# Seven block products for eight in both FFN projections of a two-layer encoder, token-major, with weight sums built by adding DMAs

## The chip, the cores and the metric

One Trainium2 chip, one core of it. The metric is device time in microseconds (us) of one execution; a kernel's time is the median of its runs. The engines named below are TensorE (PE in the profile; its weight loads are PEld), VectorE (DVE), ScalarE (ACT), GpSimd (POOL) and SyncE (SP, which issues the plain DMAs).

## The reference

A trunk of two layers on x of 512 tokens by 1024 channels, in float32. Each layer is a half-step SwiGLU FFN, a token mixer, and a second half-step FFN; a final RMSNorm ends it.

```python
def swiglu(h, w_in, w_out):                       # w_in 1024 x 5632, w_out 2816 x 1024
    gate, up = jnp.split(h @ w_in, 2, axis=-1)
    return (jax.nn.silu(gate) * up) @ w_out

for l in range(DEPTH):                            # DEPTH = 2
    x = x + 0.5 * swiglu(rms_norm(x, ffn1_norm[l]), ffn1_w_in[l], ffn1_w_out[l])
    x = x + token_mixer(rms_norm(x, mix_norm[l]), w_in[l], ...)
    x = x + 0.5 * swiglu(rms_norm(x, ffn2_norm[l]), ffn2_w_in[l], ffn2_w_out[l])
return rms_norm(x, final_norm)
```

The mixer projects x by a 1024 x 5376 matrix to three branches (pooling, differential attention, a gated linear recurrence) and their gates, merges the branches, and projects by a 1024 x 1024 matrix.

## The kernel before

Activations are channel-major: `x[m]` is 128 channels by 512 tokens. A float32 product is made of three TensorE matmuls in the 32-bit rounded type (fp32r): every operand is split into a high part (a rounding copy on ACT, `zh`, `wh`, `hh`) and a low part (source minus high part on DVE, `zl`, `wl`, `hl`), and `mm3` adds high x high, high x low and low x high into one PSUM bank.

The program is a list of **units**. A unit is 128 x 1024 weights (`raw`, loaded by SP in blocks of 128 x 2048), split into `wh` and `wl`, and the matmuls that use them: the weights are the stationary operand, 128 x 128 at a time, and the 512 tokens stream past, so a full unit has 8 x 3 = 24 matmuls of 512 columns. An FFN has 44 units for the input projection (a gate and an up tile of 128 columns in turn) and 24, some of them with 7 for 8 tiles, for the output projection. The last FFN's output projection (`final_proj`) is token-major, so that the result needs no transposing.

The order on each engine is the order in which the code emits it. After the matmuls of unit i, `gap` emits the delayed DVE work (`flush`), then the unit's own work on its result (`after`), then the ACT half of the split of unit i+3 (`splits_to`), side work of the mixer, and last the DVE half of that split, behind which the next block's DMA is issued (`loads`). So a unit's weights are split while the three units ahead of it run.

The norm factor `R` (one per token) is not applied to z but to the results; it is made from squares added up over the channel tiles and one matmul with a matrix of ones (`norm_R`, tile `nrm`).

Of the kernel before, what the change touches and what calls it, by code (L numbers as in the profile page):

```python
# [44 lines left out]
SLOTS = 72  # L45
# [3 lines left out]
SCQ = 2  # L49


class Block:
    def __init__(self, load):
        self.load = load
        self.raw = None
# [27 lines left out]
class Unit:  # L83
    def __init__(self, block, view, mm, after, nk=8, cost=5.2, shape=None):
        self.block = block
        self.view = view
        self.mm = mm
        self.after = after
        self.nk = nk
        self.cost = cost  # L90
        self.shape = shape or [8, 128]
        self.hi = self.lo = None
        self.late = 0
        self.group = 2
        self.ahead = False
# [3 lines left out]
def trunk_kernel(ctx, tc, xT, pm, fin, cst, bd, f1i, f1o, win, wbp, wba, wbl, wout, f2i, f2o, out):  # L99
    nc = tc.nc  # L100
    V, A, PE, SP = Counted(nc.vector, 0.075, 0.00104), Counted(nc.scalar, 0.14, 0.00083), Counted(nc.tensor, 0.0, 0.00042), nc.sync

    cp_ = ctx.enter_context(tc.tile_pool(name="const", bufs=1))
    sp = ctx.enter_context(tc.tile_pool(name="slots", bufs=SLOTS))
    rp = ctx.enter_context(tc.tile_pool(name="raw", bufs=3))
    wp = ctx.enter_context(tc.tile_pool(name="whl", bufs=3))
    dp = ctx.enter_context(tc.tile_pool(name="pad", bufs=2))
# [3 lines left out]
    def slot(dt=F32, name="s"):  # L111
        return sp.tile([128, S], dt, tag="s", name=name)

# [16 lines left out]
    def hilo(src, name):  # L130

        hi, lo = slot(F32R, name + "h"), slot(F32R, name + "l")
# [28 lines left out]
    x = [None] * KD  # L161
    st = {}

    def z_chunk(m, gain):

        z_split(m, gain)
        sq_chunk(m)

    def z_split(m, gain):
        zh, zl = slot(F32R, "zh"), slot(F32R, "zl")  # L170
        A.activation(out=zh, in_=x[m], func=AF.Copy, scale=gain(m))
        V.scalar_tensor_tensor(out=zl, in0=x[m], scalar=gain(m), in1=f(zh), op0=MUL, op1=SUB)
        st["z"][m] = (zh, zl)

    def sq_chunk(m):
        if m == 0:
            st["acc"] = slot(name="acc")
            A.activation(out=st["acc"], in_=x[m], func=AF.Square)
        else:
            q = slot(name="sq")  # L180
            A.activation(out=q, in_=x[m], func=AF.Square)
            V.tensor_tensor(out=st["acc"], in0=st["acc"], in1=q, op=ADD)
# [7 lines left out]

    def inv_rms(acc, n, eps, col):
        return rsqrt_newton(*inv_rms_start(acc, n, eps, col))
# [11 lines left out]
    def norm_R():  # L204
        st["R"] = inv_rms(st.pop("acc"), D, EPS, 0)

    units = []
    hooks = {}

    def add_hook(i, fn):  # L210
        hooks.setdefault(i, []).append(fn)


    def blk(pieces):
        def load(raw):
            for dst, src in pieces:
                SP.dma_start(out=dst(raw), in_=src)
        return Block(load)

    def cols_block(w, c0, n=256):  # L220
        return blk([(
            lambda raw: raw[:, 0:8 * n].rearrange("p (k f) -> p k f", f=n),
            w[:, c0:c0 + n].rearrange("(k p) f -> p k f", p=128),
        )])

    def col_view(s, n=256, k=8, c=128):
        return lambda raw: raw[:, 0:k * n].rearrange("p (k f) -> p k f", f=n)[:, :, s * c:(s + 1) * c]

    def zmm(get_bank, nk=KD, src="z"):

        def mm(u, k0, k1):
            if k0 == 0:
                get_bank(True)
            acc = get_bank(False)
            for k in range(k0, k1):
                zh, zl = st[src][k]
                mm3(acc, u.hi[:, k * 128:(k + 1) * 128], u.lo[:, k * 128:(k + 1) * 128], zh, zl, k == 0, k == nk - 1)
        return mm
# [9 lines left out]
    def ffn(l, wi, wo, next_gain, last, first=None):  # L248
        h = [None] * KF

        def pair(j, bg, bu, s):
            box, bx2 = {}, {}

            def after_gate():
                g, th = slot(name="g"), slot(name="th")
                V.tensor_tensor(out=g, in0=box["ps"], in1=st["R"], op=MUL)
                A.activation(out=th, in_=g, func=AF.Tanh, scale=0.5)
                r = st["R"]

                def rest():  # L260
                    V.scalar_tensor_tensor(out=g, in0=th, scalar=1.0, in1=g, op0=ADD, op1=MUL)
                    V.tensor_tensor(out=g, in0=g, in1=r, op=MUL)

                later.append(rest)
                box["g"] = g

            def after_up():
                g = box["g"]
                V.tensor_tensor(out=g, in0=bx2["ps"], in1=g, op=MUL)
                h[j] = hilo(g, "h")  # L270

            if bg is None:
                return (box, after_gate), (bx2, after_up)
            units.append(Unit(bg, col_view(s), zmm(new_bank_fn(box)), after_gate))
            units.append(Unit(bu, col_view(s), zmm(new_bank_fn(bx2)), after_up))

        if first is not None:
            for s in range(2):
                first.extend(pair(s, None, None, s))
        for jj in range(0 if first is None else 1, KF // 2):  # L280
            bg, bu = cols_block(wi, jj * 256), cols_block(wi, DFF + jj * 256)
            pair(2 * jj, bg, bu, 0)
            pair(2 * jj + 1, bg, bu, 1)

        if last:
            final_proj(wo, h)
            return
        kbs = [(0, 8), (8, 15), (15, KF)]
        for cg in range(4):
            blocks = []  # L290
            for k0, k1 in kbs:
                blocks.append(blk([(
                    lambda raw, n=k1 - k0: raw[:, 0:n * 256].rearrange("p (k f) -> p k f", f=256),
                    wo[k0 * 128:k1 * 128, cg * 256:(cg + 1) * 256].rearrange("(k p) f -> p k f", p=128),
                )]))
            boxes = [{}, {}]
            order = [(b, s) for b in range(3) for s in range(2)] if cg < 3 else [(b, s) for s in range(2) for b in range(3)]
            for b, s in order:
                k0, k1 = kbs[b]

                def mm(u, a0, a1, k0=k0, k1=k1, box=boxes[s]):
                    if k0 == 0:
                        box["ps"] = bank()
                    for k in range(k0, k1):
                        o = (k - k0) * 128
                        mm3(box["ps"], u.hi[:, o:o + 128], u.lo[:, o:o + 128], h[k][0], h[k][1], k == 0, k == KF - 1)

                def after(m=2 * cg + s, box=boxes[s], fin=b == 2):
                    if not fin:
                        return  # L310
                    if m == 0:
                        st["z"] = [None] * KD
                    V.scalar_tensor_tensor(out=x[m], in0=box["ps"], scalar=0.25, in1=x[m], op0=MUL, op1=ADD)
                    z_chunk(m, next_gain)

                n = k1 - k0
                units.append(Unit(blocks[b], col_view(s, 256, n), mm, after, nk=n, cost=0.65 * n, shape=[n, 128]))


    def final_proj(wo, h):  # L320
        xt, gain, xg = {}, {}, {}
        ss = {t: small(2) for t in range(4)}

        def prepare():
            for ch in range(2):
                gain[ch] = slot(name="fg")
                SP.dma_start(out=gain[ch], in_=fin[ch * S:(ch + 1) * S].partition_broadcast(128))
            yield 0.1, lambda: None, True
            for ch in range(2):
                for t in range(4):  # L330
                    def step(ch=ch, t=t):
                        ps = bank("xt")
                        for k in range(4):
                            PE.transpose(ps[:, k * 128:(k + 1) * 128], x[ch * 4 + k][:, t * 128:(t + 1) * 128], ident)
                        xt[t, ch] = slot(name="xt")
                        A.activation(out=xt[t, ch], in_=ps, func=AF.Copy)
                    yield 0.7, step, True

        add_hook(len(units) - 4 * (KF // 2) + 4, lambda: side.add("xt", prepare()))

        def close(t, ch, ps):
# [20 lines left out]
        for ch in range(2):  # L362
# [3 lines left out]
            for j in range(nu):  # L366
# [7 lines left out]
                def mm(u, a0, a1, j=j, ch=ch, box=box, nu=nu):  # L374
# [3 lines left out]
                    if ch == 1 and nu - tail <= j < nu - 1:  # L378
                        return
# [851 lines left out]
```

## Time and profile before

| | |
|---|---|
| median of 3 runs | 2199.44 us (2199.42 to 2199.46) |
| profiled execution, its own time | 2199.48 us |
| its span in the trace | 2197.5 us |
| TensorE busy | 2181.1 us, 99% of the span |
| VectorE busy | 1243.3 us, 57% |
| ScalarE busy | 819.6 us, 37% |
| DMA | 207 MB, 28.7% of the 16 engines' time |
| granted TensorE clock, mean | 0.999 (2.4 GHz) |

The span is what the engines' rows cover; about 2 us of the execution lie around it. Matmuls are pipelined: a row of 0.39 us follows the one ahead of it by less than that, so the cost of a matmul is read from the distance of starts, not from a row's length. Idle time of an engine that others don't wait for costs nothing.

### The profile page before, as it was taken

To read this page: it belongs to the slowest core of one execution; us is meant where nothing else is said; L and a number is where in the kernel's file an instruction comes from. 1 tells how busy PE (TensorE), PEld (TensorE's weight loads), DVE (VectorE), ACT (ScalarE), POOL (GpSimd) and SP (SyncE) were. 2 spreads that over 40 slices of the span, in tenths; PEclk is the share of its full clock that TensorE was granted. 3 is DMA by queue.
4 is the path that set the end of the run, shared out by engine and by line. 5 is a ranking of instruction groups with operands and counts; after the bars stand their busy time and mean duration, and the time that the engine had idled before them with its cause. 6 is when DMAs were issued, how large, how long until landed. Compare 5 with 4: busy or idle time off the path is not lost.

```text
span 2197.5 us, 23345 instructions
## 1 busy us (share of the span) xinstructions
PE 2181.1 (99%) x9596; PEld 1786.2 (81%) x9596; DVE 1243.3 (57%) x1743; ACT 819.6 (37%) x1137; POOL 0.2 (0%) x4
## 2 busy tenths in 40 slices
PE   9999999999999999999999999999999999999998
PEld 7888888778887888888888888877788878888887
DVE  6655434697866655543355554346977675555433
ACT  5322223645654322222232222246456443322222
POOL 0000000000000000000000000000000000000000
PEclk9999999999999999999999999999999999999999
DMA  5323232222223222232232323232222233232331
GB/s 185 113 79 115 86 103 92 96 67 87 77 68 106 96 96 96 96 106 91 91 99 93 108 84 106 87 120 73 70 87 68 89 103 106 77 115 79 113 104 50
DMA packets 193610, 207.44 MB, mean 94 GB/s; under 512 B 3808, under 2 KB 183136, under 8 KB 193504
## 3 DMA queue, kind: packets, MB, share of 16 engines
q1 hardware_dynamic: 193504, 205.96, 28.7%
q8 instruction: 75, 1.23, 0.2%
q14 instruction: 31, 0.25, 0.0%
HBM read 203.85 MB, written 2.10 MB: 94 GB/s over the span
## 4 chain that ended last, share of the span: by engine, by line
PE 87%; DVE 9%; ACT 3%; issue 1%; DMA 0%; SPq 0%; ACTq 0%; DVEq 0%
PE ps L78 74%; PE f L78 5%; PE y L78 2%; PE v L78 2%; DVE wl L78 2%; PE av L78 1%; DVE gt L78 1%; ACT wh L78 1%; PE sc L78 1%; DVE hs L78 1%; DVE tl L78 1%; DVE kl L78 1%; PE wT L78 0%; PE nrm L78 0%; DVE pw L78 0%
## 5 line engine op out<-in xcount | busy, mean ns | idle before, releaser
L78 PE MATMUL ps<-zh,wh 128*128 128x512 f32 x2016 | 793.5, 394 | 0.4 <-DVE m L78 0.2
L78 PE MATMUL ps<-zh,wl 128*128 128x512 f32 x2016 | 786.0, 390 | 2.3 <-DVE wl L78 2.0
L78 PE MATMUL ps<-zl,wh 128*128 128x512 f32 x2016 | 784.7, 389 | 0.0
L78 DVE TENSOR_TENSOR wl<-raw,wh 128x1024 fp32r<-128x1024 f32 (+1 forms) x382 | 459.8, 1206 | 289.7 <-ACT wh L78 286.3
L78 ACT ACTIVATE wh<-raw 128x1024 fp32r<-128x1024 f32 (+1 forms) x382 | 394.8, 1036 | 291.2 <-PE ps L78 171.2
L78 PEld LDWEIGHTS ps<-zh,wl 128*128 128x128 f32 x2016 | 378.4, 188 | 85.1 <-DVE wl L78 6.0
L78 PEld LDWEIGHTS ps<-zh,wh 128*128 128x128 f32 x2016 | 378.5, 188 | 82.2 <-issue 3.4
L78 PEld LDWEIGHTS ps<-zl,wh 128*128 128x128 f32 x2016 | 378.6, 188 | 81.2 <-issue 3.8
L78 PE MATMUL ps<-hh,wh 128*128 128x512 f32 x528 | 205.4, 389 | 0.0
L78 PE MATMUL ps<-hl,wh 128*128 128x512 f32 x528 | 205.4, 389 | 0.0
L78 PE MATMUL ps<-hh,wl 128*128 128x512 f32 x528 | 205.4, 389 | 0.0
L78 ACT ACTIVATE hh<-g 128x512 fp32r<-128x512 f32 x88 | 55.6, 632 | 325.0 <-DVE g L78 325.0
L78 ACT ACTIVATE th<-g 128x512 f32<-128x512 f32 x88 | 55.6, 632 | 324.7 <-DVE g L78 324.7
L78 DVE TENSOR_TENSOR g<-ps,r 128x512 f32<-128x512 f32 x88 | 60.8, 691 | 151.1 <-PE ps L78 151.0
L78 DVE TENSOR_TENSOR g<-ps,g 128x512 f32<-128x512 f32 x88 | 60.9, 691 | 118.6 <-PE ps L78 118.1
L78 PEld LDWEIGHTS ps<-hh,wl 128*128 128x128 f32 x528 | 99.1, 188 | 20.7
L78 PEld LDWEIGHTS ps<-hl,wh 128*128 128x128 f32 x528 | 99.1, 188 | 20.6
L78 PEld LDWEIGHTS ps<-hh,wh 128*128 128x128 f32 x528 | 99.1, 188 | 20.4
L78 DVE SCALAR_TENSOR_TENSOR g<-th,g 128x512 f32<-128x512 f32 x88 | 61.0, 693 | 59.9 <-ACT th L78 59.8
L78 DVE TENSOR_TENSOR hl<-g,hh 128x512 fp32r<-128x512 f32 x88 | 61.0, 693 | 59.1 <-ACT hh L78 59.0
L78 ACT ACTIVATE gt<-gt,hmb 128x512 f32<-128x512 f32 x48 | 34.8, 724 | 135.3 <-DVE gt L78 131.4
L78 ACT ACTIVATE zh<-x,par 128x512 fp32r<-128x512 f32 x48 | 34.6, 721 | 134.2 <-DVE x L78 134.2
(172 smaller groups left out, 1972.6 us busy)
## 6 DMA issues: line engine op xcount, KB each, us to landing
raw<-in_f2i_dram SPq DMA_DIRECT2D x44, 1024.0 KB, 4.9
raw<-in_f1i_dram SPq DMA_DIRECT2D x42, 1024.0 KB, 4.9
raw<-in_win_dram SPq DMA_DIRECT2D x42, 1024.0 KB, 5.1
raw<-in_f1o_dram SPq DMA_DIRECT2D x16, 896.0 KB, 4.8
raw<-in_f2o_dram SPq DMA_DIRECT2D x14, 1024.0 KB, 5.0
raw<-in_f1o_dram SPq DMA_DIRECT2D x8, 1024.0 KB, 5.1
raw<-in_wout_dram SPq DMA_DIRECT2D x8, 1024.0 KB, 5.0
raw<-in_f2o_dram SPq DMA_DIRECT2D x8, 896.0 KB, 4.8
```

The costliest lines, as they stand in the source:

```text
L78: return fn(*args, **kw)
```

## The change

**Block products.** Each FFN projection is cut into 2 x 2 blocks (the tokens in halves, the summed dimension in halves, and the output columns in halves: gate and up in the input projection, channels 0 to 511 and 512 to 1023 in the output projection), and the eight block products are replaced by seven (Winograd's form of Strassen's scheme): `P1 = A11 B11`, `P2 = A12 B21`, `Q5 = S1 (B11+B12)`, `Q3 = S4 B22`, `P6 = S2 (B11+B12+B22)`, `P7 = S3 (B12+B22)`, `Q4 = A22 (B11+B12+B22+B21)`, with signs as the code has them. S1 to S4 are sums and differences of activation blocks, made on DVE. The sums of weight blocks are built in SBUF by DMAs that add to what lies there (`add_fn`, issued by GpSimd): one tile holds B11, then B11+B12, then B11+B12+B22, and then all four.

**Token-major.** The activations are now the stationary operand (128 channels by 128 tokens of a half) and 512 columns of weights stream past. A unit is still 128 x 1024 weights, but feeds 2 token tiles x 2 weight tiles x 3 = 12 matmuls, half as many as before. The input projection goes through 2816 columns in six steps (`quad`): five of 512 columns, with 7 products of 2 units each, and one of 256 columns, with 7 products of one unit each, of 24 matmuls of 256 columns. The output projection has 7 products of 6 units (the sixth half as long).

**Combining.** The products are added up on DVE and ACT as they end (`p1` to `q4` in `quad`, `o_p1` to `o_q4` behind it), tanh is taken token-major with the norm factor as a scalar per partition, and h is transposed on TensorE (`transposes`, tile `ht`) to be stationary in the output projection. x stays token-major; z is transposed from it on TensorE (`z_block`, `z_chunk`, tile `zt`). The norm factor comes from ACT squares with a running sum, without a matmul. `final_proj` and its transposes are gone, since every output projection is now token-major.

The core of the diff, in the new kernel's form:

```diff
-SLOTS = 72
+SLOTS = 20
+BIGS = 40
...
+    def add_fn(src, n, w):
+        return lambda raw: GP.dma_start(out=raw[:, 0:n * w].rearrange("p (k f) -> p k f", f=w), in_=src, accum_op=ADD)
...
+    def seven(order, nk, width, left, wap, after, chain2, held, prep=None):
...
+                if p == "P1":
+                    block = b1[n] = Block([ld(0, 0)])
+                    acc = ap(0, 1)
+                elif p == "Q5":
+                    block, acc = b1[n], ap(1, 1)
+                elif p == "P6":
+                    block, acc = b1[n], ap(1, 0)
+                elif p == "Q4":
+                    block = b1[n]
+                elif p == "P2":
+                    block = Block([ld(1, 0)])
+                elif p == "Q3":
+                    block = b2[n] = Block([ld(1, 1)])
+                    acc = ap(0, 1) if chain2 else None
+                else:
+                    block = b2[n] if chain2 else Block([ld(0, 1)], ap(1, 1))
...
+                    for tt in range(2):
+                        acc_ = box[p][tt][:, 0:width]
+                        for k in range(k0, k1):
...
+                            PE.matmul(acc_, lhsT=ah, rhs=wh, start=k == 0, stop=False)
+                            PE.matmul(acc_, lhsT=ah, rhs=wl, start=False, stop=False)
+                            PE.matmul(acc_, lhsT=al, rhs=wh, start=False, stop=k == nk - 1)
...
+            def p6(ps):
+                def rest():
+                    for tt in range(2):
+                        add(u[tt], ps[tt], u[tt])
+                        add(v[tt], v[tt], u[tt], SUB)
+                        mul(v[tt], v[tt], st["r"][tt][2], th0[tt])
...
+                later.append(rest)
+                defer(2, transposes(0, v))
...
         def low():
-            V.tensor_tensor(out=lo, in0=src, in1=f(hi), op=SUB)
-            if last_use[id(u.block)] == i:
+            for lo, src, hi in todo:
+                V.tensor_tensor(out=lo, in0=src, in1=hi, op=SUB)
...
+            if u.acc:
+                u.acc(u.block.raw[0])
+            elif last_use[id(u.block)] == i:
...
+            loads()
```

`chain2` is true in the input projection and false in the output projection. `u.acc` is called behind the DVE half of a unit's split: the add may only start when both halves of the split have read the tile, and the unit four places on in a 512-column step (two places on in the 256-column step, twelve in the output projection) reads the sum.

DVE in an FFN's input projection. Before, this is the row for one pair of units (gate, then up), from one eviction of a gate tile to the next:

```order
L78 TENSOR_TENSOR g<-ps,r 128x512 [waits PE_49]
L78 SCALAR_TENSOR_TENSOR g<-th,g 128x512 [waits Activation_49]
L78 TENSOR_TENSOR g<-g,r 128x512 [waits DVE_49]
L78 TENSOR_TENSOR wl<-raw,wh 128x1024 [waits Activation_49]
L78 TENSOR_TENSOR g<-ps,g 128x512 [waits DVE_49,PE_49]
L78 TENSOR_TENSOR hl<-g,hh 128x512 [waits Activation_49]
L78 TENSOR_TENSOR wl<-raw,wh 128x1024 [waits DMAHW0_49,Activation_49]
```

Two splits (`wl`) come with five other operations, for 48 matmuls. Now, in a 512-column step, the stretch behind product P6 (`u<-P_826`) and then P7 (`u<-P_870`):

```order
L83 TENSOR_TENSOR u<-P_826,u 128x512 [waits PE_49]
L83 TENSOR_TENSOR v<-v,u 128x512 [waits DVE_49]
L83 SCALAR_TENSOR_TENSOR v<-v,m,th 128x512 [waits DVE_49]
L83 TENSOR_TENSOR u<-P_827,u 128x512 [waits PE_49]
L83 TENSOR_TENSOR v<-v,u 128x512 [waits DVE_49]
L83 SCALAR_TENSOR_TENSOR v<-v,m,th 128x512 [waits DVE_49]
L83 TENSOR_TENSOR wl<-raw,wh 128x1024 [waits DMASW6_49,Activation_49]
L83 TENSOR_TENSOR wl<-raw,wh 128x1024 [waits DMASW7_49,Activation_49]
L83 TENSOR_TENSOR u<-P_870,u 128x512 [waits PE_49]
L83 TENSOR_TENSOR u<-u 128x512 [waits DVE_49]
```

Six dependent operations now stand between the end of a product and the split of a unit three places on, and that split waits for an adding DMA (`DMASW`). In the output projection DVE has, behind product P2 (`x<-P_2370`), the sums `c` of h blocks, their low parts `al`, and the splits of the weights in one row:

```order
L83 TENSOR_TENSOR c_2424<-h 128x1024 [waits PE_49]
L83 TENSOR_TENSOR c_2425<-c_2424,h 128x1024 [waits DVE_49]
L83 TENSOR_TENSOR wl<-raw,wh 128x512 [waits DMAHW7_49,PE_49,Activation_49]
L83 TENSOR_TENSOR al<-c_2424,ah 128x1024 [waits Activation_49]
L83 TENSOR_TENSOR wl<-raw,wh 128x1024 [waits DMASW4_49,PE_49,Activation_49]
L83 TENSOR_TENSOR c_2467<-h 128x1024 [waits PE_49]
L83 TENSOR_TENSOR c_2468<-c_2467,h 128x1024 [waits DVE_49]
L83 TENSOR_TENSOR wl<-raw,wh 128x1024 [waits DMASW5_49,Activation_49]
L83 SCALAR_TENSOR_TENSOR x<-P_2370,x 128x512 [waits PE_49]
```

Before, DVE had only the splits and the additions to x there; the five rows with `c` and `al` are new, and the splits wait for loads and adds. The third place is GpSimd's queue, which issues the adding DMAs. Before, it held no DMA; now, at the 256-column step of the first FFN, it has one chain of three adds to the tile `raw_1520` and one add to `raw_1612`, one unit per product:

```order
L366 DMA raw_1520<-in_f1i_dram 128x4x256 [waits DMAHW1_49,DVE_49]
L366 DMA raw_1520<-in_f1i_dram 128x4x256 [waits DMASW0_49,DVE_49]
L366 DMA raw_1612<-in_f1i_dram 128x4x256 [waits DMAHW3_49,DVE_49,PE_49]
L366 DMA raw_1520<-in_f1i_dram 128x4x256 [waits DMASW1_49,DVE_49]
L366 DMA raw_1640<-in_f1o_dram 128x2x512 [waits DMASW4_49,DMAHW4_49,DVE_49,PE_49]
```

Each add waits for the one ahead of it in its tile and for DVE, which has read the tile for the split. In all there are 272 such adds, 68 to an FFN, four of them in its narrow step.

## Rows read from the trace of the kernel before

**Rows 1.** The page: engines' busy time and the chain that ended last.

```profile
PE 2181.1 (99%) x9596; PEld 1786.2 (81%) x9596; DVE 1243.3 (57%) x1743; ACT 819.6 (37%) x1137; POOL 0.2 (0%) x4
PEclk9999999999999999999999999999999999999999
...
PE 87%; DVE 9%; ACT 3%; issue 1%; DMA 0%; SPq 0%; ACTq 0%; DVEq 0%
```

**Rows 2.** Waits of PE, the largest: total us, times, longest.

```profile
PE ps L78 <- DVE wl L78: 2.5, 5, 0.7
```

**Rows 3.** Windows: FFN 2 of layer 0 (input, output projection), then a mixer.

```profile
738.00:976.00 238.00, 238.00 (x1049) 196.37 (x1048) 130.44 (x158) 72.15 (x91) 0.00 (x0) 1.00 0.30 97
976.00:1096.00 120.00, 120.00 (x531) 99.38 (x530) 42.61 (x47) 32.20 (x39) 0.00 (x0) 1.00 0.30 99
...
1460.00:1824.00 364.00, 360.43 (x1583) 290.38 (x1582) 266.04 (x428) 189.84 (x286) 0.00 (x0) 1.00 0.26 83
```

**Rows 4.** Timeline of PE: start us, length; 21 matmuls, then the norm's.

```profile
368.23 0.39 PE L78 MATMUL ps<-zh,wh 128*128 128x512 f32 x1
...
372.76 0.39 PE L78 MATMUL ps<-zh,wl 128*128 128x512 f32 x1
372.99 1.02 PE L78 MATMUL nrm<-acc,cst 128*128 128x512 f32 x2
...
374.09 0.40 PE L78 MATMUL ps<-zl,wh 128*128 128x512 f32 x1
```

**Rows 5.** Timeline of PE around eight transposes, then around four.

```profile
506.72 1.03 PE L78 MATMUL wT<-cst,e 128*128 128x128 f32 x8
...
507.82 0.40 PE L78 MATMUL ps<-zl,wh 128*128 128x512 f32 x1
...
1865.44 0.60 PE L78 MATMUL xt<-cst,x 128*128 128x128 f32 x4
...
1866.11 0.39 PE L78 MATMUL ps<-zl,wh 128*128 128x512 f32 x1
```

**Rows 6.** Lines by shape, weight loads and transposes: busy us, mean ns.

```profile
L78 PEld LDWEIGHTS ps<-zh,wl 128*128 128x128 f32 x2016 | 378.4, 188 | 85.1 <-DVE wl L78 6.0
L78 PE MATMUL wT<-cst,e 128*128 128x128 f32 x128 | 16.6, 272 | 0.0
L78 PEld LDWEIGHTS wT<-cst,e 128*128 128x128 f32 x128 | 14.9, 140 | 2.1
```

**Rows 7.** Lines by shape: DVE and ACT.

```profile
L78 DVE TENSOR_TENSOR wl<-raw,wh 128x1024 fp32r<-128x1024 f32 x334 | 407.3, 1222 | 184.5 <-ACT wh L78 181.5
L78 ACT ACTIVATE wh<-raw 128x1024 fp32r<-128x1024 f32 x334 | 349.3, 1049 | 182.1 <-PE f L78 73.1 <-PE ps L78 62.0 <-issue 15.4
L78 DVE TENSOR_TENSOR g<-ps,g 128x512 f32<-128x512 f32 x88 | 60.9, 691 | 118.6 <-PE ps L78 118.1
L78 DVE SCALAR_TENSOR_TENSOR zl<-x,par,zh 128x512 fp32r<-128x512 f32 x48 | 36.0, 750 | 36.6 <-ACT zh L78 36.6
L78 ACT ACTIVATE th<-g 128x512 f32<-128x512 f32 x88 | 55.6, 632 | 324.7 <-DVE g L78 324.7
```

**Rows 8.** The page: DMA; queue's MB and share of engines; us to landing.

```profile
DMA packets 193610, 207.44 MB, mean 94 GB/s; under 512 B 3808, under 2 KB 183136, under 8 KB 193504
q1 hardware_dynamic: 193504, 205.96, 28.7%
...
raw<-in_f2i_dram SPq DMA_DIRECT2D x44, 1024.0 KB, 4.9
raw<-in_wba_dram SPq DMA_DIRECT2D x8, 512.0 KB, 3.4
```

**Rows 9.** Timeline: PE's first product, and its last.

```profile
6.67 0.42 PE L78 MATMUL ps<-zh,wh 128*128 128x512 f32 x1
...
2190.04 0.39 PE L78 MATMUL f<-wh,hl 128*128 128x512 f32 x1
```

More of the change, by code (lines that the diff above doesn't have):

```diff
@@ L158, in pcs, with add_hook, defer @@
         return par[:, o:o + PCOLS[name][1]]
[L161 to L182, printed above, removed]
+    x = {}
+    st = {"r": {}}
+    units = []
+    hooks = {}
+    tasks = {}
+    clock = {"gap": 0}
+    def add_hook(i, fn):
+        hooks.setdefault(i, []).append(fn)
+    def defer(n, fn):
+        tasks.setdefault(clock["gap"] + n, []).append(fn)
     def rsqrt_newton(y0, m):
@@ new lines, in to_ffn, with done, to_mixer @@
+    def to_ffn(gain):
+        def done(hh, kk):
+            squares(hh, kk)
+            defer(1, z_block(hh, kk, gain))
+            z_ready(hh, kk, 2)
+        return done
+    def to_mixer(gain):
+        got = set()
+        def done(hh, kk):
+            squares(hh, kk)
+            got.add((hh, kk))
+            if kk == 1 and (1 - hh, 1) in got:
+                st["z"] = [None] * KD
+                for c2 in range(2):
+                    defer(1 + c2, lambda c2=c2: [z_chunk(4 + 2 * c2 + c, gain) for c in range(2)])
+        return done
@@ new lines, in to_out, with close @@
+    def to_out(hh, kk):
+        both = squares(hh, kk)
+        if not both:
+            for tt in range(2):
+                xv = x[2 * hh + tt, kk]
+                V.tensor_tensor(out=xv, in0=xv, in1=st["fg"][kk], op=MUL)
+            return
+        def close():
+            for tt in range(2):
+                t = 2 * hh + tt
+                r = st["r"][t][0]
+                A.activation(out=x[t, 1 - kk], in_=x[t, 1 - kk], func=AF.Copy, scale=r)
+                V.scalar_tensor_tensor(out=x[t, kk], in0=x[t, kk], scalar=r, in1=st["fg"][kk], op0=MUL, op1=MUL)
+                for c in (1 - kk, kk):
+                    SP.dma_start(out=out[t * 128:(t + 1) * 128, c * S:(c + 1) * S], in_=x[t, c])
+        later.append(close)
@@ L401, in mixer @@
+    def mixer(l, side, done, between):
         g = {}
@@ L887, in mixer @@
         units[-4].ahead = True
[L890 to L901 removed]
+        units[n0].late = units[n0 + 1].late = 4
@@ L938, in trunk_kernel, with prologue @@
     side = Side()
-    def prologue(first, w):
+    def prologue(gain):
         SP.dma_start(out=par, in_=pm)
+        SP.dma_start(out=cs[:, 0:256], in_=cst[:, 0:256])
         warm = slot(F32R, "warm")
@@ L1064, in trunk_kernel, with between @@
-    blocks = []
-    for u in units:
-        if not blocks or all(b is not u.block for b in blocks[-4:]):
+    for l in range(DEPTH):
+        g1, gm, g2 = (lambda m, n=n, l=l: pc(l, n, m) for n in ("g1", "gm", "g2"))
+        order0 = ["P1" if l == 0 else "P2", "P2" if l == 0 else "P1", "Q5", "Q3", "P6", "P7", "Q4"]
+        ffn(f1i[l], f1o[l], to_mixer(gm), order0)
+        def between(gm=gm):
+            for m in range(4):
+                z_chunk(m, gm)
+            flush()
+        mixer(l, side, to_ffn(g2), between)
+        last = l == DEPTH - 1
+        n = len(units)
+        ffn(f2i[l], f2o[l], to_out if last else to_ffn(lambda m, l=l: pc(l + 1, "g1", m)), ["P2", "P1", "Q5", "Q3", "P6", "P7", "Q4"])
+        if last:
+            add_hook(len(units) - 44, load_gains)
@@ L1067, in trunk_kernel, with loads @@
+    blocks, last_use = [], {}
+    for i, u in enumerate(units):
+        if u.block and id(u.block) not in last_use:
             blocks.append(u.block)
-    last_use = {}
-    for i, u in enumerate(units):
         last_use[id(u.block)] = i
-    state = {"dma": 0, "split": 0, "held": 0}
-    def loads():
-        while state["dma"] < len(blocks) and state["held"] < 3:
+    state = {"dma": 0, "split": 0, "held": 0, "lim": 8}
+    def loads(lim=None):
+        while state["dma"] < len(blocks) and state["held"] + len(blocks[state["dma"]].loads) <= (lim or state["lim"]):
@@ L1115, in gap @@
             u = units[i]
+            state["lim"] = u.held
             V.t, A.t = max(V.t, PE.t), max(A.t, PE.t)
-            u.after()
-            u.hi = u.lo = None
-            for fn in hooks.get(i, []):
+            if u.after:
+                u.after()
+            u.hi = u.lo = u.mm = u.after = None
+        for fn in tasks.pop(clock["gap"], []):
+            fn()
+        for i in done:
+            for fn in hooks.pop(i, []):
                 fn()
@@ L1124, in gap @@
         side.gap += 1
+        clock["gap"] += 1
         for fn in lows:
```

801 lines of the change are left out of this document (486 added, 315 removed).

## The prediction

> **What bounds the kernel now.** I read the page first: TensorE is busy for 99% of the span at the full clock (granted 0.999, the 2.4 GHz level), VectorE for 57%, ScalarE for 37%, and the chain that ended last is 87% TensorE [rows 1]. Then the waits of TensorE: the largest is 2.5 us in total [rows 2], so there is no wait to remove. The windows by stage show it in each stage; an FFN takes 358 us here, DVE has 173 us of work in it, and ACT 104 us [rows 3]. So the time falls only by as much as TensorE has less to do, and only as far as the engines behind it keep up. The pace is read from starts: 21 matmuls of 512 columns begin between 368.23 and 372.76, 0.2265 us apart [rows 4].
>
> **TensorE's work after.** An FFN had 44 x 24 + 22 x 8 x 3 = 1584 matmuls of 512 columns. Now the input projection has 5 steps x 14 units x 12 = 840 of them and 7 x 24 = 168 of 256 columns, the output projection 7 x 11 x 2 x 3 = 462 of 512. Four FFNs: 1128 fewer at 0.2265, **-255.5 us**, and 672 narrow ones more. No row has a matmul of 256 columns. Half of 0.2265 is 0.113 (76 us in all); the weight load's row is 0.188 [rows 6] (126 us), but the transposes, whose loads have rows of 0.140 [rows 6], run faster than that (next sentence), so the row overstates the pace by about 0.03. I take 0.13, near the lower end: **+87 us**. Eight transposes take 507.82 - 506.72 - 0.2265 = 0.87 us, four take 0.44 [rows 5]: 0.11 each, all told. There are 4 x (88 + 32) for h and z, 64 for the mixers' z and 8 for the norm factor, less 40 that go: 512 x 0.11 = **+56.3 us**. Six norm matmuls go, each 374.09 - 372.99 - 0.2265 = 0.87 us [rows 4]: **-5.2 us**. TensorE's sum is **-117.4 us**; an FFN is then 5 steps of 39.8 us, one of 22.7, 104.6 for the output projection and 3.5 for z, about 330 us.
>
> For the narrow matmuls the Trainium skill (TensorE: Matmul & The Clock Gate, Back-to-back issue gap) gives 262 cycles, 0.109 us at 2.4 GHz, and 0.216 for 512 columns, which the rows here exceed by 5%. By it, as an estimate, the sum would be 14 us lower.
>
> **What DVE and ACT must do behind it.** A split costs 1.222 us on DVE and 1.049 on ACT [rows 7] and now feeds 12 matmuls, 2.72 us, for 5.44 before. A wide step has 14 splits (17.1 us) and 22 operations of 512 columns, 18 at 0.691 and 4 with a pointer scalar at 0.750 [rows 7]: 32.5 of 39.8 us. The narrow step: 7 splits and 22 operations of 256 columns, 0.43 each on the line through the 512 and 1024 rows: 17.9 of 22.7. The output projection: splits 47.6, four sums and seven low parts of 2816 columns 37.4, additions 15.2: 100.2 of 104.6 us. The seven z operands: 11 x 1.222 = 13.4 us, nearly all in the first step. Together 294 of 330 us. ACT stays lower (a wide step: 14 x 1.05 + 12 x 0.63 = 22 of 39.8). So on the sums DVE still fits, but not everywhere.
>
> The lookahead decides where. The split of unit i+3 is emitted behind unit i, so it must be done two units later, 5.44 us. In a wide step the worst stretch is behind P6: six operations and a split, 5.5 us, against 5.44 plus eight transposes of 0.88: no stall. In the **first step** of an FFN four gaps in a row carry S1 to S4 and their low parts, 4.9 + 3.7 + 5.0 + 3.8 = 17.4 us, against 4 x 2.72 + 2.72 = 13.6: about 4 us late, **16 us** for four FFNs (0 to 30). In the **output projection** ten gaps from the first `c` carry 28.9 us against 24.5 + 2.7: 2 us, **8 us** in all (0 to 20). At the **mixers** the last z tiles wait for the last product, an addition, transposes and a split, about 3.3 us; 24 matmuls (5.4 us) lie over that, and the tiles then come singly: 2 us twice, **4 us**.
>
> **The adding DMAs.** No row shows one. It moves a 512 KB tile that it also has to read in SBUF. A load of 512 KB lands after 3.4 us [rows 8], the lower bound; a load of 1024 KB after 4.9; two loads of 512 KB in a row would be 6.8, which I take as the upper end. I take 6, since it queues behind the loads. In a wide step a sum is read four units (10.9 us) after the tile was split; a link is the add and a split (1.05 + 1.22), so it is free up to 8.6 us. In the narrow step the distance is two units (6.2 us): three links of 6 + 2.3, with 2.5 ahead, end at 27.4 against 4 x 6.2 = 24.8: about 3 us late, **12 us** for four (0 at 4.9 us, 20 at 6.8). In the output projection the distance is twelve units, and the loads run four ahead.
>
> For this time the Trainium skill (DMA: Bandwidth & Descriptors, Anatomy of one DMA) gives 2.0 us plus the bytes at 436 GB/s for a DMA issued by GpSimd: 3.2 us, for a plain copy. By it the 12 us fall away.
>
> **Start and end.** Before, the first product starts at 6.67 us, and 7.1 us follow the last matmul [rows 9]. Now eight transposes, an ACT copy of a whole z block and its split come ahead of the first product: **+4 us** (2 to 8). The end has one product's rows more to add: **+1 us**. The mixers' own work is unchanged; their splits are cut in two (2 x 0.69 for 1.22 on DVE, 12 us over both), which the 27% that DVE idles there [rows 3] covers.
>
> **Sum.** 2197.5 - 117.4 + 16 + 8 + 4 + 12 + 5 = 2125 us of span; with the 2 us that lie around it (the profiled 2199.48 is also the median) **2127 us**, 3.3% faster. Its own range, by the bounds, is 2075 to 2190.
>
> **Rivals.**
> *All of it hides* (narrow matmuls at 0.113, no stall): 2127 - 11 - 40 = 2076. For it: no engine but TensorE is full on the sums. Against it: the first step's sum is over.
>
> *The DMAs become the bound* (the other side). All transfers took 28.7% of 16 engines for 206 MB [rows 8]: 3.06 us of all engines per MB, 1.6 us for a tile. A wide step has 14 tiles, 22.5 of 39.8 us, an output projection 70.6 of 104.6 us; 8 of 14 and half of the latter are adds. If an add costs w loads, a step takes 9.6 + 12.8 w and the output projection 35.3 (1 + w). At w = 2 that is 35 and 106 us: just full. At w = 3 the excess is 8 us a wide step, 1 the narrow one and 37 the output projection, 79 us an FFN; it takes the place of the stalls: about 2127 - 36 + 318 = 2409. It is slower than before from w = 2.4. For it: the bytes nearly double and an add reads two places and writes one. Against: rows of 2 KB for 1 KB now, and 94 GB/s in the mean before [rows 8], far from full.
> The Trainium skill's same page (Issuing engines are not separate DMA queues) says that DMAs of all queues share the 16 engines; by that rule adds on GpSimd's queue gain no room, which is what this rival needs. No run here shows it yet.
>
> *DVE becomes the bound.* Its 294 of 330 us leave 36. If each of the 119 units leaves DVE idle for 0.6 us because its operand comes from ACT, DVE needs 365 us, and the time is 2127 - 28 + 140 = 2239; slower from 0.5 us. For it: such waits are the rule now (a low part behind its high part). Against: they are idle time of a free engine; a full one finds its operands ready.
>
> *The change doesn't relieve TensorE.* If narrow matmuls go at the weight load's 0.188 and transposes at their rows' 0.272 [rows 6], 39 + 83 us are added: 2249. Against it: rows 5.
>
> **Chances.** The forecast 0.52, all hidden 0.15, DMA-bound 0.20, DVE-bound 0.10, TensorE not relieved 0.03. A difference under 0.2% (2195 to 2204) can't be told from none. Faster: 0.52 + 0.15 and 0.03 of the DVE case, 0.70; same: 0.02 of that case; slower: the rest, 0.28. The range that leaves 2 in 10 out is 2075 to 2250: it cuts most of the DMA case above and half of the hidden one below.
>
> **What would show it.** PE busy near 2065 to 2080 us and the distance of narrow starts (0.13) and of transposes (0.11) test the first term. PE's waits should be for `wl`, 10 us or less per FFN, in the first step, the narrow step and the output projection; DVE near 290 us in an FFN. An add should land in about 6 us. The prediction is wrong if the splits `wh` wait for adding DMAs in wide steps, if the DMA share in FFNs stands at 9 tenths or more, or if PE is idle through the output projections while DVE is full.

## The result and the profile after

The changed kernel takes 2215.45 us (median of four runs, 2214.34 to 2216.77), the kernel before 2199.45 on the same chip: a ratio of 1.0073 (95% interval 1.0055 to 1.009), 0.7% slower. Forecast were 2127 us. The profiled span is 2212.2 us.

The page of the changed kernel: TensorE's busy time, the granted clock and the DMA share by slice, the DMA queues (packets, MB, share of the 16 engines), the chain that ended last, and the time from issue to landing of three kinds of DMAs (an adding one, a load, an adding one).

```profile
PE 2106.6 (95%) x9640; PEld 1723.0 (78%) x9640; DVE 1656.1 (75%) x2327; ACT 1186.4 (54%) x1735; POOL 325.7 (15%) x276
...
PEclk9999999999999999999999999999999999999999
DMA  9789697123125287878967878951222344779795
...
q0 software_dynamic: 76032, 138.43, 36.9%
q1 hardware_dynamic: 121872, 182.90, 25.4%
...
PE 52%; DMA 21%; DVE 12%; issue 8%; ACT 6%; POOL 2%; SPq 0%; POOLq 0%; ACTq 0%; DVEq 0%
...
raw<-in_f1i_dram POOLq DMA_DIRECT2D x88, 512.0 KB, 7.4
...
raw<-in_f2i_dram SPq DMA_DIRECT2D x66, 512.0 KB, 5.0
...
raw<-in_f1o_dram POOLq DMA_DIRECT2D x40, 512.0 KB, 8.6
```

TensorE has 74.5 us less busy time than before [rows 1], but it is no longer busy for 99% of the span, and its share of the chain has fallen from 87% to 52%; 21% are now DMAs. The queue of the adding DMAs takes 36.9% of the engines' time for 138 MB, the loads 25.4% for 183 MB. TensorE's own waits (total us, times, longest):

```profile
PE P L83 <- ACT wh L83: 31.7, 10, 7.2
PE Q L83 <- DVE wl L83: 17.6, 22, 1.6
PE P L83 <- DVE wl L83: 17.1, 29, 1.2
PE Q L83 <- ACT wh L83: 11.8, 10, 2.8
```

The high parts `wh` are late, not only the low parts `wl`. What ScalarE waits for when it makes `wh`:

```profile
ACT wh L83 <- DMA raw<-in_f2i_dram: 166.9, 65, 8.7
ACT wh L83 <- DMA raw<-in_f1i_dram: 153.6, 62, 8.7
```

Both are weight tiles that are still being loaded or added to. The windows of the second FFN of layer 0 (its 512-column steps, its 256-column step, its output projection) and, last, the end of the first output projection, with PE, PEld, DVE, ACT and POOL busy, the clock, the DMA share (a window counts the whole time of the packets that start in it, so it can pass 1) and GB/s:

```profile
752.30:965.10 212.80, 204.08 (x923) 165.24 (x922) 159.35 (x190) 112.39 (x143) 48.36 (x40) 1.00 0.80 170
965.10:996.50 31.40, 24.82 (x182) 23.11 (x180) 17.31 (x26) 13.82 (x20) 5.15 (x4) 0.95 0.65 130
996.50:1115.80 119.30, 111.08 (x493) 90.28 (x492) 102.17 (x118) 71.70 (x100) 27.84 (x24) 0.97 0.89 206
340.00:362.00 22.00, 14.32 (x53) 11.01 (x52) 11.20 (x18) 9.89 (x15) 1.93 (x2) 0.80 1.08 284
```

TensorE is idle for 9, 7 and 8 us in the first three (before, it was busy in all of such a stretch [rows 3]), although the DMA engines are not full in the mean of any of them (0.80, 0.65, 0.89). They are full at the end of an output projection (1.08), where 22 us hold 14 us of TensorE's work and the granted clock is 0.80. The chain that ended last, in order of time (start, length, what):

```profile
90.05 13.02 DMA raw<-in_f1i_dram
...
130.98 13.44 DMA raw<-in_f1i_dram
...
172.59 11.02 DMA raw<-in_f1i_dram
...
212.71 11.81 DMA raw<-in_f1i_dram
231.02 6.11 DMA raw<-in_f1i_dram
239.82 6.13 DMA raw<-in_f1i_dram
...
248.59 6.98 DMA raw<-in_f1i_dram
...
328.81 10.47 DMA raw<-in_f1o_dram
339.83 15.65 DMA raw<-in_f1o_dram
357.87 6.69 PE P L83 x17
```

This chain goes through adding DMAs, the longest of 11 to 13 us, in the 512-column steps (their starts are those of GpSimd's issues), through three adds one behind the other in the 256-column step, and through a load and an add, 10.47 and 15.65 us, at the end of the output projection. Rows of the timeline from each of the three places, and what stands around them (start, length, engine, operation; in brackets the idle time before it and what ended it):

```profile
88.92 2.44 POOL L366 DMA_DIRECT2D raw<-in_f1i_dram  x2 [2.88 <-DVE wl L83]
...
230.39 0.28 PE L83 MATMUL P<-wh,zh 128*128 128x256 f32 x1
...
231.02 1.30 POOL L366 DMA_DIRECT2D raw<-in_f1i_dram  x1 [17.10 <-DVE wl L83]
...
237.21 1.06 ACT L83 ACTIVATE wh<-raw 128x1024 fp32r<-128x1024 f32 x1 [8.68 <-DMA raw<-in_f1i_dram]
238.17 0.64 ACT L83 ACTIVATE u<-P 128x256 f32<-128x256 f32 x2
...
349.01 0.39 PE L83 MATMUL P<-wh,al 128*128 128x512 f32 x1
...
355.50 1.06 ACT L83 ACTIVATE wh<-raw 128x1024 fp32r<-128x1024 f32 x1 [10.58 <-DMA raw<-in_f1o_dram]
...
356.61 0.80 PE L83 MATMUL P<-wh,ah 128*128 128x512 f32 x1 [7.21 <-ACT wh L83]
```

At 88.92 GpSimd issues two adds in a row: the second is the one of 13.02 us. At 230.39 the 256-column step begins on TensorE, and only at 231.02, behind the low part `wl` of its first tile, can GpSimd issue its first add. At 237.21 ScalarE has waited 8.68 us for an add, and the copies of product P1 behind it in its queue (`u<-P`) have waited too. At 355.50 it is 10.58 us; the two PE rows are 7.6 us apart, and the second is 0.80 us long where a row at the full clock has 0.39.

### The profile page after: what moved, and what is told of

Read it like the earlier page. It is cut to its first block, busy times and chain, and to the rows that moved or that the text cites. A ratio compares the mean times of both kernels' runs of the same rounds, so it can differ in the third digit from the quotient of the medians.

```text
span 2212.2 us, 25981 instructions
## 1 busy us (share of the span) xinstructions
PE 2106.6 (95%) x9640; PEld 1723.0 (78%) x9640; DVE 1656.1 (75%) x2327; ACT 1186.4 (54%) x1735; POOL 325.7 (15%) x276
## 3 DMA queue, kind: packets, MB, share of 16 engines
q0 software_dynamic: 76032, 138.43, 36.9%
q1 hardware_dynamic: 121872, 182.90, 25.4%
## 4 chain that ended last, share of the span: by engine, by line
PE 52%; DMA 21%; DVE 12%; issue 8%; ACT 6%; POOL 2%; SPq 0%; POOLq 0%; ACTq 0%; DVEq 0%
PE ps L83 17%; PE P L83 11%; DMA raw<-in_f1i_dram 9%; PE Q L83 9%; DMA raw<-in_f2i_dram 7%; DVE wl L83 6%; PE o L83 4%; PE y L83 4%; ACT wh L83 3%; DMA raw<-in_f1o_dram 2%; POOL raw L366 2%; PE v L83 1%; PE sc L83 1%; DMA raw<-in_f2o_dram 1%; PE av L83 1%
## 5 line engine op out<-in xcount | busy, mean ns | idle before, releaser
L83 DVE TENSOR_TENSOR wl<-raw,wh 128x1024 fp32r<-128x1024 f32 (+1 forms) x668 | 705.4, 1076 | 294.3 <-ACT wh L83 291.1
L83 PE MATMUL ps<-z,wh 128*128 128x512 f32 x1216 | 380.2, 393 | 0.0
L83 PE MATMUL P<-wl,zh 128*128 128x512 f32 (+1 forms) x768 | 291.8, 380 | 13.0 <-DVE wl L83 12.7
L83 PE MATMUL P<-wh,zh 128*128 128x512 f32 (+1 forms) x768 | 290.6, 378 | 9.6 <-ACT wh L83 9.6
L83 PE MATMUL P<-wh,zl 128*128 128x512 f32 (+1 forms) x768 | 288.5, 376 | 0.0
L83 PEld LDWEIGHTS ps<-z,wh 128*128 128x128 f32 x1216 | 227.1, 188 | 51.0 <-issue 3.4
L83 PE MATMUL Q<-wl,zh 128*128 128x512 f32 (+1 forms) x576 | 221.1, 384 | 17.0 <-DVE wl L83 17.0
L83 PE MATMUL ps<-z,wl 128*128 128x512 f32 x608 | 237.0, 390 | 0.0
L83 PE MATMUL Q<-wh,zh 128*128 128x512 f32 (+1 forms) x576 | 220.5, 383 | 12.0 <-ACT wh L83 11.8
L83 PE MATMUL Q<-wh,zl 128*128 128x512 f32 (+1 forms) x576 | 217.5, 378 | 0.6 <-DVE zl L83 0.6
```

The costliest lines, as they stand in the source:

```text
L83: return fn(*args, **kw)
```

## The experiments

Each ran beside the kernel before, which took 2199.36 to 2199.66 us on the chips used. The time is the median of the runs (one run each for "no adds" and "plain copies"); the span and the stages are those of the one profiled execution. The table has the length of each stage, from its first product's first matmul in the timeline to the next stage's (of the last output projection, to its last matmul): the 512-column steps of the four FFNs, the sum of the four 256-column steps, and of the four output projections. The two mixers are 742 us in every one of them. "Both" is the narrow sums on GpSimd and the one chain together.

| kernel | time | span | 512-column steps | 256-column | output |
|---|---|---|---|---|---|
| changed | 2215.45 | 2212.2 | 219.0, 212.8, 209.7, 212.9 | 126.7 | 468.6 |
| no adds | 2112.08 | 2110.3 | 216.5, 205.4, 204.1, 205.4 | 85.6 | 430.4 |
| plain copies | 2126.76 | 2124.6 | 218.0, 205.4, 204.1, 205.4 | 95.1 | 433.9 |
| narrow sums on GpSimd | 2189.19 | 2184.9 | 218.3, 211.7, 209.9, 210.6 | 102.6 | 468.6 |
| one chain in the output | 2173.36 | 2168.9 | 216.9, 210.5, 207.0, 211.3 | 125.6 | 434.0 |
| both | 2154.83 | 2150.3 | 218.9, 211.4, 207.6, 210.1 | 105.1 | 433.5 |
| both, start | 2149.85 | 2147.5 | 218.4, 209.5, 208.7, 210.4 | 104.0 | 433.5 |
| both, splits ahead | 2156.96 | 2157.8 | 218.2, 215.3, 208.0, 212.7 | 105.3 | 433.5 |
| both, start and ahead | 2156.27 | 2158.1 | 219.9, 215.0, 209.1, 212.4 | 105.0 | 433.6 |
| late mixer loads | 2205.13 | 2201.8 | 218.8, 211.5, 208.4, 210.9 | 123.8 | 465.5 |

My theory after the result: the adding DMAs are late, and all else is as forecast. The rival: VectorE and ScalarE, in order and three quarters full, are the bound, and the adds only end at the same time.

### No adds

```diff
-                if b.acc:
-                    b.acc(raw)
...
             if u.acc:
-                u.acc(u.block.raw[0])
+                pass
```

> No adding DMA is issued: every product reads the weight tile that its first load left there (the sums of weight blocks are left out of the computation; loads, splits, matmuls and all other work are the changed kernel's). By the theory that the lost time is the adding DMAs', waits of about 42 us in the narrow steps, 38 us in the last products of the output projections, some 15 us in the wide steps and 10 us at the start go: 2212 - 105 = about 2107 us of span, 2095 to 2125, and TensorE's waits that are left are for VectorE in the first steps (about 20 us). By the rival that VectorE's and ScalarE's in-order work is the bound and the adds only end at the same time, the time stays above 2185 us.

Measured: a span of 2110.3 us, 101.9 less. The page (TensorE, clock, the loads' queue), the windows of the same three stages, and two matmuls of the 256-column step, 30 apart:

```profile
PE 2071.3 (98%) x9640; PEld 1710.3 (81%) x9640; DVE 1656.4 (78%) x2327; ACT 1183.8 (56%) x1735; POOL 0.2 (0%) x4
...
PEclk8999999999999999999999999999999999999999
...
q1 hardware_dynamic: 121872, 182.90, 26.5%
```

```profile
728.60:934.00 205.40, 201.11 (x923) 165.79 (x922) 162.36 (x192) 112.82 (x144) 0.00 (x0) 1.00 0.23 73
934.00:955.40 21.40, 21.40 (x182) 21.39 (x180) 18.39 (x29) 13.04 (x19) 0.00 (x0) 1.00 0.24 83
955.40:1064.10 108.70, 108.51 (x493) 89.51 (x491) 98.41 (x112) 71.28 (x99) 0.00 (x0) 1.00 0.37 122
```

```profile
934.84 0.28 PE L83 MATMUL P<-wl,zh 128*128 128x256 f32 x1
...
938.44 0.28 PE L83 MATMUL P<-wl,zh 128*128 128x256 f32 x1
```

VectorE does as much work as with the adds (1656.4 us for 1656.1; 162 and 98 us in the first and the last of these stages) and TensorE hardly waits: the rival falls. Of the 101.9 us, 41.1 lie in the 256-column steps, 38.2 in the output projections and 23.0 in the 512-column steps, for the 42, 38 and 15 expected. The further 10 us expected at the start aren't there: the first FFN's 512-column steps lose 2.5 us to the adds, the other three 20.5. The matmuls of 256 columns start 0.12 us apart (3.60 us for 30).

### Plain copies

```diff
-        return lambda raw: GP.dma_start(out=..., in_=src, accum_op=ADD)
+        return lambda raw: GP.dma_start(out=..., in_=src)
```

> Each adding DMA is replaced by a plain copy of the same 512 KB from the same place to the same tile, from GpSimd's queue and behind the same waits (the sums are left out of the computation). If adding itself is what costs 5.90 us of all 16 engines per MB, where loads cost 3.07, the share of GpSimd's queue falls from 36.9% to about 19%, a copy lands in about 4.5 us for 6.1 to 8.7, and the time falls to about 2130 us (2110 to 2150). If it is GpSimd's queue that costs, whatever the DMA does, the share stays at 35% or more, landings at 6 us or more, and the time within 15 us of the 2215 us of the changed kernel.

Measured: 2124.6 us of span, as the first case has it. The queue of GpSimd, and the landings of its copies (7.4 us as adds):

```profile
q0 software_dynamic: 38144, 138.43, 19.3%
...
raw<-in_f1i_dram POOLq DMA_DIRECT2D x88, 512.0 KB, 4.7
```

The same 138.43 MB go through the same queue behind the same waits, and its share is 19.3% for 36.9%. An add takes 0.369 x 2212.2 / 138.43 = 5.90 us of all engines per MB, a copy 0.193 x 2124.6 / 138.43 = 2.96, a load 3.07: adding costs 1.99 copies. It is adding, not GpSimd's queue, that loses 87.6 of the 101.9 us; the other 14.3 go with the copies too, 9.5 of them in the 256-column steps.

### The narrow step's sums on GpSimd

```diff
+        if width < S:
+            whole = Block([load_fn(wap(r, c, 0, nk), nk, width) for r, c in ((0, 0), (1, 0), (0, 1), (1, 1))])
+            psum = lambda a, b: lambda raw: GP.tensor_tensor(out=whole.raw[a], in0=whole.raw[a], in1=whole.raw[b], op=ADD)
...
+                    acc = {"P1": psum(0, 2), "Q5": psum(0, 3), "Q3": psum(3, 2), "P6": psum(0, 1)}.get(p)
```

> Only in the narrow step of each input projection: the four weight blocks are loaded plainly, and GpSimd adds them up in SBUF as 128x1024 additions, in place of four adding DMAs. No row shows how long GpSimd takes for one; on VectorE it is 1.22 us. If the links of the narrow step (an add of 6.1 us, a split of 2.3 us and the waits between, 8.8 us, against two products of 2.9 us each) are the cause, and GpSimd needs less than 3.5 us, the 42 us lost there fall to 10 or less: about 2183 us (2175 to 2190), faster than the kernel before. If the narrow step waits for VectorE and ScalarE, or GpSimd needs 6 us too, 2210 us or more.

Measured: 2189.19 us, a ratio of 0.9957 (0.9942 to 0.9971) to the kernel before. The four steps fall from 126.7 to 102.6 us, 17.0 above those without adds, where 10 or less were expected. GpSimd's additions by line, and the timeline around the second of them:

```profile
L415 POOL TENSOR_TENSOR raw<-raw 128x1024 f32<-128x1024 f32 x16 | 44.1, 2759 | 95.4 <-DVE wl L83 95.4
```

```profile
235.43 2.81 POOL L415 TENSOR_TENSOR raw<-raw 128x1024 f32<-128x1024 f32 x1 [2.43 <-DVE wl L83]
...
236.01 2.77 DVE L83 SCALAR_TENSOR_TENSOR u<-u,m,th 128x512 f32<-128x512 f32 x1
...
239.43 0.75 DVE L83 SCALAR_TENSOR_TENSOR u<-u,m,th 128x512 f32<-128x512 f32 x1
```

A link is now 2.76 + 2.3 us, less than two products, so the links are free. Of the 17.0 us, TensorE waits for 12.0 in the four steps, all of them for VectorE (`wl` and `u`), whose operation at 236.01 takes 2.77 us where the same one at 239.43 takes 0.75; it ends just behind GpSimd's addition.

### One chain of adds in the output projection

```diff
-              {"P1": o_p1, ..., "P7": o_p7, "Q4": o_q4}, False, 10, prep)
+              {"P1": o_p1, ..., "P7": o_p7, "Q4": o_q4}, True, 12, prep)
```

> Only in the output projections: product P7's weights are made by one add to the tile that Q3 has read, where the changed kernel loads one more tile and adds to it: 24 loads fewer, and the adds start one product earlier. If the DMA engines are full there with 12 adds and 14 loads behind P6, the 38 us that the last products lose fall to about 10: 2187 us (2178 to 2197). If the mixer's loads, which come in a burst of eight, are what the adds wait behind, the wait moves to Q4 and the time stays within 10 us of 2215.

The last value of the edit, 12 for 10, is the number of tiles that may be held while the projection runs; it was not tried by itself. Measured: 2173.36 us, a ratio of 0.9883 (0.9868 to 0.9897), more than expected: 34.6 us in the output projections, and 8.7 in the 512-column steps, which the expectation doesn't have. All four output projections are within 2 us of those without adds. The window of the one that stands above:

```profile
978.10:1088.50 110.40, 109.00 (x493) 89.37 (x491) 102.12 (x118) 71.38 (x100) 27.81 (x24) 1.00 0.90 204
```

The DMA share in the mean is the same as with the waits, 0.90 for 0.89. So the mean was not what counted. In the first output projection the last add of 512 KB is issued at 326.58 us, where it was 339.83 in the changed kernel; it still takes 14.07 us, and no `wh` of that projection waits for an add by more than 0.3 us. So the last adds have to be issued while there are products left to cover them; how much of the gain is the 24 loads that go was not told apart.

### Was it the mixer's burst of loads?

```diff
-                units.append(Unit(..., acc=acc, held=held, nk=k1 - k0))
+                units.append(Unit(..., acc=acc, held=6 if held == 10 and p == "P7" else held, nk=k1 - k0))
```

> The changed kernel, but while P7's units of an output projection run, tiles of the next stage are loaded only when fewer than six tiles are held, where it was ten: the mixer's (or the next projection's) first loads, a burst of eight in the changed kernel, come after P7's last adds. If that burst is what made the last add take 15.7 us, the output projections, 119, 119, 118 and 112 us, fall to about 110 us: 2215 - 27 = 2188 us (2180 to 2196). If their own 12 adds and 6 loads behind P6 fill the DMA engines by themselves, they fall by 3 us or less each, and the next stage starts with late loads: 2205 us or more.

Measured: 2205.13 us (ten runs from 2197.08 to 2209.85), a ratio of 1.002 (1.0006 to 1.0034). The burst now starts behind the issue of the last adds, though while they are under way; the chain's row for the add that ended the wait, and the loads' row:

```profile
338.62 14.47 DMA raw<-in_f1o_dram
```

```profile
341.22 14.67 SPq L363 DMA_DIRECT2D raw<-in_win_dram  x8
```

The add still takes 14.47 us, for 15.65. When it is issued, three others of 512 KB and one of 256 KB are still to land ahead of it; with itself they need 4.5 x 0.524 x 5.90 = 14 us of all engines, an estimate from the price of an add above that leaves the burst little to answer for. The output projections fall by 2.3, 0.6 and 3.1 us and the last one grows by 2.9, 3.1 us in all: the burst's part is small, and the rival, the projection's own transfers, holds. The other 7 us by which the span is shorter lie in the input projections and were not explained.

### Both, and two more

> Both changes that each took away one place of the waits: the narrow steps' sums on GpSimd and one chain of adds in the output projections. If the two places are independent, the gains add: from the spans 2212.2, 2184.9 and 2168.9 us, 2168.9 - 27.3 = 2142 us of span, 2144 us of time (2138 to 2150). If the waits only move to the next place where transfers are late (GpSimd's queue, full with its additions, holds up the adds of the output projection), 2155 us or more.

Measured: 2154.83 us, a ratio of 0.9797 (0.9782 to 0.9811). Neither expectation was met in full: the sum of the gains would be a span of 2141.6 us, and it is 2150.3. The output projections keep their gain (433.5 us). The 256-column steps would be 101.5 by the sum and are 105.1, and the 512-column steps, which had gained 3.9 and 8.7 us in the two kernels by the way, gain 6.4 and not 12.6. These two make up the difference of 8.7, so no wait has moved into the output projections; which of it is more than the scatter of runs (2152.07 to 2157.38) was not tried.

```diff
-            n += 2
+            n += 1
             loads(n)
-        SP.dma_start(out=cs[:, 256:NCST], in_=cst[:, 256:NCST])
-        loads(8)
+        add_hook(12, lambda: SP.dma_start(out=cs[:, 256:NCST], in_=cst[:, 256:NCST]))
...
+        loads(6)
...
-    state = {"dma": 0, "split": 0, "held": 0, "lim": 8}
+    state = {"dma": 0, "split": 0, "held": 0, "lim": 6}
```

> As the kernel with both changes, and at the start one weight tile is loaded ahead for each 128x512 pair of x in place of two, six in place of eight before the first products, and the large table of constants is loaded 12 units later. If the full DMA engines (98% or more from 6 to 24 us) make the first adds late (9.8 to 11.9 us to landing), the first input projection, 217 us from its first product for 205 to 211 in the others, falls by 5 to 8 us and the first product starts up to 1 us earlier: 2136 us (2132 to 2141). If the start waits for the order of the work on ScalarE and VectorE, no difference of more than 2 us from the kernel with both changes.

Measured: 2149.85 us, a ratio of 0.9775 (0.976 to 0.979) to the kernel before, 2.3% faster. Its interval overlaps that of the kernel with both changes alone, and the first 512-column steps are as long as ever (218.4 us for 218.9), so the start's DMAs are not what makes them long. They are 216.5 us even without adds, 11 us more than in the other FFNs, all of it in the first step (56.7 us for 44.5 to 45.8). Of that, the trace without adds shows 6.8 us of clock, granted at 0.50 (the 1.2 GHz level) for 13.6 us of the first step and at 1.00 in the others, and 2.8 us or more of longer idle time of TensorE.

```diff
+        if n0:
+            for u in units[n0 + 1:n0 + 6]:
+                u.ahead = True
```

> As the kernel with both changes, and in the first step of the last three input projections ScalarE and VectorE split the weights ahead of the sums S1 to S4 of the same gap, where the changed kernel does it behind them. If the waits of 5.3 to 6.6 us a step that are left there without any add are for weight splits that queue behind the sums (VectorE works without a pause for 12 us there), half of them go: 8 to 10 us over three steps, 2135 us (2131 to 2139). If VectorE's sum is over the time of the products in that step whatever its order, the waits move to the operands S1 to S4 and the time stays within 3 us.

Measured: 2156.96 us, a ratio of 0.9805 (0.979 to 0.982). TensorE's waits with both changes alone, and then with the splits ahead:

```profile
PE Q L83 <- DVE wl L83: 13.8, 18, 1.6
```

```profile
PE Q L83 <- ACT zh L83: 11.9, 4, 4.3
...
PE Q L83 <- DVE wl L83: 2.3, 5, 1.3
```

The wait for `wl` goes and one for `zh` takes its place, 3.4 to 4.3 us in one piece, and `zh` waits for VectorE's sums: in this step VectorE's sum is over the products' time whatever its order, as the rival has it. Without adds TensorE idles 3.4 to 4.3 us in each of these steps, less than the 5.3 to 6.6 of the expectation, so there was less to gain. Behind the new wait the granted clock is 0.50 for some 6.7 us in each of the three steps (from 1104.3 to 1111.0 us, for one), where it stayed at 1.00 with both changes alone.

> Both further changes at once, at the start and in the first steps: they touch different places, so the gains add: about 2128 us (2122 to 2136), if each does what is expected of it alone; the kernel with both changes' own time, if neither does.

Measured: 2156.27 us, a ratio of 0.9802 (0.9785 to 0.9818): neither gives a gain on top that can be told from none.

## Why the prediction was wrong

**TensorE's work** was right. Without adds its busy time is 2071.3 us, inside the 2065 to 2080 given as the sign. In the changed kernel it is 2106.6 with the same matmuls: some 15 of the 35 us more are the clock (below), the rest was not followed. Narrow matmuls start 0.12 us apart for 0.13, so the term was 7 us too high, and the rival that TensorE isn't relieved (0.188) falls. The Trainium skill's 0.109 (TensorE: Matmul & The Clock Gate, Back-to-back issue gap), which stands there for one matmul by itself, is a tenth too low here.

**VectorE and ScalarE** were right: VectorE has 159 + 17 + 102 = 279 us in the three windows of an FFN, for the forecast 294. The first steps' waits are there (3.4 to 4.3 us of idle TensorE in those of the last three FFNs without adds, for 4), and the output projections without adds are 107.2 to 108.8 us, for 106.6. The VectorE-bound rival falls with the run without adds.

**Everything but the adds** sums up: the forecast span of 2125 us less its 12 for adds is 2113, and without adds the span is 2110.3. What failed is the price of the adds, **12 us forecast and 101.9 measured**, in three steps. The range of 2075 to 2250 holds the measured time, but by luck: only the rivals' prices made it so wide, and none of its cases has adds that are late while the DMA engines are not full in the mean.

*The narrow step, 12 us forecast, 41 measured.* The add itself is right: those at 231.02 and 239.82 take 6.1 us, and the links are 8.8 us apart, for 8.3. What failed is "with 2.5 ahead", the split that starts the chain. The forecast has it done 2.5 us after it could start, which is 3.7 us before its product begins; so three links stand against 4 x 6.2. In all four steps it ended 0.2 to 1.0 us behind its product's first matmul (the rows at 230.39 and 231.02). Without adds and with plain copies it ends 2.6 us before. The last add of the 512-column step ahead (212.71, 11.81 us) was late, and the splits behind it moved by the same 2.9 us. So the forecast's slack was gone at the start: three links of 8.8 us against three distances of 5.8 (two products of 24 matmuls at 0.12) are 9 us a step. Measured are 10.3, with the clock that falls behind the waits. The stages were added up as if each began on time; the lateness of one was the start of the next.

*The output projection's adds, nothing forecast, 38 us measured.* "The distance is twelve units, and the loads run four ahead" holds for the chain of four sums, not for P7, whose tile is loaded and then added to. The load of the last such tile is issued at 328.81 and takes 10.47 us, the add behind it 15.65, and ScalarE asks for the sum at 355.50 - 10.58 = 344.92, 16 us after the load's issue. The DMA rival had the right price ("at w = 2 ... just full"; it is 1.92 loads) and spread it over the whole projection, so that it decided only from w = 2.4 (2.5 by its own terms, as the excess takes the place of the stalls). The transfers aren't spread: from 320 to 360 us stand 10 adds and the loads of 4.2 MB, 109% of the engines. With one chain instead, the same mean share costs next to nothing (3.6 us over the four).

*The wide steps, nothing forecast, 23 us measured.* "Free up to 8.6" is right as a bound, and the median landing of 7.4 to 7.9 us is under it; but of the 160 adds of these steps 65 took more than 8.6 us to land, the longest 14.4, behind others at a share of 0.8. One time for all adds was used where the late ones count. Plain copies at the same places cost nothing in the last three FFNs.

The sign was named beforehand: `wh` that waits for DMAs in wide steps, and a DMA share of 9 tenths (0.89 in the output projection). **The clock** was left out as well. It was 0.999 in the mean before, is 0.985 now and 0.996 without adds; rows at the half clock stand behind waits of several us, as at 356.61. In the FFNs the matmuls that start at about twice their usual distance cost some 21 us over that distance in the changed kernel's timeline and 6 without adds: some 15 of the 101.9 us, over and above the waits themselves.

The Trainium skill has such a price where the prediction didn't look (Collectives: The Full Stack, The bandwidth ceiling: the fold count and why AG ≠ RS ≠ AR): the add of a reduce-scatter needs two source reads where an all-gather's copy needs one, and goes at half the rate, 1.93 measured there. The trace agrees: an add is 1.92 loads or 1.99 copies here. A plain copy from GpSimd's queue lands in 4.5 to 5.1 us here (512 KB, medians by tensor), not in the 3.2 us by which the prediction's 12 us would have fallen away.

## What to carry to other kernels

Price a DMA that adds at two plain ones, and ask for the stretch between two reads of the tile, product by product, whether the adds that become ready there fit into it; a mean share over a stage doesn't show it. A chain of adds to one tile loses the difference of link and distance at every link, and the slack at its start is what pays for it: ask whether the stage ahead leaves that slack. Where adds come late, change when they can be issued (one more reuse of a tile that has been read, which here saved a load as well).

## What the runs showed of the hardware

An add has twice the packets of a copy of the same bytes: 76032 for 138.43 MB, 38144 as plain copies, and a packet takes the same time in both, 0.17 us of one engine (0.369 x 2212.2 x 16 / 76032 and 0.193 x 2124.6 x 16 / 38144). GpSimd is busy for 325.7 / 276 = 1.18 us with issuing an add (four of the 276 are not adds). Loads that SyncE issues land later beside the adds: 7.7 us (in_f1i, median) for 3.4 without them.

While GpSimd adds two tiles in SBUF, an operation of VectorE can stand until it ends (0.75 us became 2.77); over the kernel, 44.1 us of such additions added 23 us to VectorE's busy time (1679.6 for 1656.1). The Trainium skill (SBUF — State Buffer, Summary: rules for kernel authors) states that where VectorE has two inputs in SBUF while GpSimd reads SBUF, the second to issue blocks until the first ends; the trace agrees.

The kernels with adds don't repeat as well: the kernel before lay within 1 us in 13 runs, the one with the late mixer loads within 13 in ten.
